# A hybrid attention and recurrence block: output gates computed in pairs, and sums and low parts of weights made by adding DMAs

## The chip, the cores and the metric

The kernel runs on one core of a Trainium2 chip. The core has four compute engines that run side by side, each with its own list of instructions executed in order: TensorE (PE, matrix products, results into eight PSUM banks), VectorE (DVE), ScalarE (ACT) and GpSimd (POOL). A fifth, SyncE (SP), issues DMAs here; ACT and POOL issue some too, and the DMA engines carry them out. An engine waits for another by a semaphore, and while its first instruction waits, everything behind that on the same engine waits with it. The metric is the time of one execution in microseconds (us); less is better.

## The reference

One layer over T = 528 tokens (16 learned ones and 512 of the input), width D = 2048, all in float32. In short:

```python
h = rms_norm(concat([meta, x]), norm_g)
q_a,k_a,v_a,z_a, q_i,k_i,w_i, q_b,f_b,i_b,z_b, gates = split(h @ w_in)
# branch A: an indexer scores keys per query, the top 128 are attended to
score = sum_h(relu(rope(q_i)_h @ rope(rms_norm(k_i))) * w_i_h)
sel   = top_k(where(chunk(key) <= chunk(query), score, -inf), 128)
y_a   = softmax_attention(rope(rms_norm(q_a)), rope(rms_norm(k_a)), v_a, sel) * silu(z_a)
# branch B: a gated linear recurrence (HGRN2), in chunks of 64
y_b   = rms_norm(hgrn2(silu(q_b), f, i_b)) * silu(z_b)
p     = stack([y_a, y_b]) @ w_branch            # per branch
out   = x + sum(sigmoid(gates) * p, branches) @ w_out
```

The product with `w_in` (2048 by 12368) is the largest piece, then `w_branch` and `w_out`.

## The kernel before

**Products.** TensorE takes float32 rounded to fewer bits (type fp32r). So each operand is split into a rounded high part and the low rest, and a product is three matmuls: high by high, high by low, low by high (`mm3`, L1606). Activations `hH`, `hL` stay in SBUF, 16 tiles each (one per 128 of D). Weights stream: SP loads chunks of 512 KB into six `raw` buffers; `hi_lo` (L402) makes `wh` on ACT (a rounding copy) and `wl` = `raw` − `wh` on DVE, three buffers of each. The number behind a name, as in `wh18`, counts chunks.

**Order of the work.** A head (L1616 on) loads x, normalises each block of 128 tokens (`norm_x`, L498: squares on ACT and DVE, a power on POOL), transposes it on PE (`px`), and makes `hH`, `hL`; with them run the first two jobs, kiwi (keys and weights of the indexer, 80 columns) and q_i block 0. While x arrives, PE runs 33 transposes of the identity into a bank `pw` that nobody reads.

Then *classical* blocks (`Job("in")`): 128 output columns, 16 tiles of D, three matmuls of 512 tokens each, 48 in all, weights in two chunks of 8 tiles. Before the change they are kiwi, eight q_i blocks and four z_a blocks (`NZA` = 4; z_a are the output gates of attention): chunks 0 to 25.

Then *pairs* (`run_pair`, L1263): two blocks of 128 columns at once by the seven-product scheme of Winograd and Strassen on halves of D and of the tokens. A pair has seven products of 24 matmuls of 256 (or 272) tokens, 168 in all; its weights are four chunks and sums of them: `s3` and `s4` by adding DMAs that POOL issues, `s2` and `s1` by DVE. The activations need sums too: `tops_task` (L1189) makes per pair of tiles k and 8+k `r1` = `hH`+`hL` and `r2` on DVE, then five more DVE sums and the splits into `tT`. `place_t3` (L1221) at last overwrites half of `hH`, `hL` with a sum and its low part. Pairs are, in order: 16 for HGRN, 2 for the other four z_a, 8 for attention, 16 for the merge gates. Then come branch jobs (32, `pg` at L95 with `yH`, `yL`) and output pairs (`po`).

**What sets the order.** Each engine's list is fixed when the program is written. Background work (the indexer's scores `psc`, `rl`, `score`; top-k; the tops; HGRN; attention) is written as generators, `tasks`. `pump` (L226) is called after each tile of a block and steps those whose planned ready time (`E.clk`, a rough model of the engines) has come, by priority, if SBUF slots (71, `room`) and PSUM banks (`bank`, `pair`) are free. `finish(t)` (L238) instead steps everything until `t` is done, without regard to what PE has to do meanwhile. It is called for the tops at the last classical block, ahead of its matmuls; behind that block's first chunk stands `place_t3`.

A score: PE makes `psc` from `kkH`, `kkL` and `qst` (a q_i block after its rotation on DVE and its split), ACT applies relu into `rl`, DVE adds it, weighted, to `score`. Each half block has four `psc` tiles of 144, 272, 400 and 528 keys; the last takes the one pair of banks. Each q_i block needs its own result first: ACT copies it (`xqi`), DVE rotates it (`qpx`, `qxc`), ACT and DVE split it into two `qst`.

In an attention head, `qa_task` (L826) ends with four exponentials and four scalings on ACT in one go, then `pv_task` (L896) multiplies with V. At the end of the last pair `finish_y`, `load_y` and `split_y` fetch the outputs `y` of branch B (`ORDER[0]` = 1) by eight ACT DMAs (`yr`) and split them (`yH` on ACT, `yL` on DVE).

Of the kernel before, what the change touches and what calls it, by code (L numbers as in the profile page):

```python
# [40 lines left out]
NZA = 4  # L41
# [144 lines left out]
def hybrid_kernel(ctx, tc, x, meta, vecs, w_in, rows, w_branch, w_out,  # L186
# [215 lines left out]
    def hi_lo(k, src, m, then=None, lazy=False):  # L402
        h = wp.tile([128, 1024], F32R, name=f"wh{k}", tag=f"wh{k % NWS}")
        l = wp.tile([128, 1024], F32R, name=f"wl{k}", tag=f"wl{k % NWS}")
        E.act(h[:, :m], src, AF.Copy)

        def lo():
            (E.ptt if k < 6 else E.tt)(l[:, :m], src, h[:, :m].bitcast(F32), OP.subtract)
            if then:
                then()  # L410

        if lazy:
            pend.append(lo)
        else:
            lo()
        return h, l

    def split_chunk(k, ch):
        load_upto(ch["i"])
        m = ch["nk"] * ch["ncols"]  # L420
        r, nk, n = ch["raw"], ch["nk"], ch["ncols"]
        ch["h"], ch["l"] = [], []
        if k < 4:
            for g in range(2):
                h, l = slot("eh", F32R), slot("el", F32R)
                w = 4 * n
                E.act(h[:, :w], r[:, w * g:w * g + w], AF.Copy)
                (E.ptt if k else E.tt)(l[:, :w], r[:, w * g:w * g + w], h[:, :w].bitcast(F32), OP.subtract)
                early.extend((h, l))
                ch["h"] += [h[:, n * i:n * i + n] for i in range(4)]  # L430
                ch["l"] += [l[:, n * i:n * i + n] for i in range(4)]
        else:
            h, l = hi_lo(k, r[:, :m], m)
            ch["h"] = [h[:, n * i:n * i + n] for i in range(nk)]
            ch["l"] = [l[:, n * i:n * i + n] for i in range(nk)]
        load_upto(ch["i"] + NRAW)
# [389 lines left out]
    def qa_task(h, xq, prev):  # L826
# [59 lines left out]
        yield e  # L886
        E.dve([sm], [sm], 4, lambda vv: vv.reciprocal(sm.rearrange("p (q i) -> p q i", i=4)[:, :, 3],
                                                      sm.rearrange("p (q i) -> p q i", i=4)[:, :, 2]))
        for qt in (3, 2, 1, 0):
            xs = ps[qt]  # L890
            e = E.act(xs[:, :KQ[qt]], xs[:, :KQ[qt]], AF.Copy, scale=col(qt, 3))
        pv_tasks.append(spawn(pv_task(h, ls, ps, e), 1))
# [3 lines left out]
    def pv_task(h, ls, ps, e):  # L896
# [23 lines left out]
        for b in (3, -1, 0, 1, 2):  # L920
# [32 lines left out]
            if b == 1:  # L953
# [234 lines left out]

    def tops_task():  # L1189
# [3 lines left out]
        for k in range(8):  # L1193
            yield from room(8 - k % 2)
            if k % 2 == 0:
                t3 = slot("t3")
            r1, r2, t1, c = slots("tr", 4)
            d = t3[:, 256 * (k % 2):256 * (k % 2) + 256]
            E.tt(r1[:, :512], hH[k][:, 16:528].bitcast(F32), hL[k][:, 16:528].bitcast(F32), OP.add)
            yield E.tt(r2[:, :512], hH[8 + k][:, 16:528].bitcast(F32), hL[8 + k][:, 16:528].bitcast(F32), OP.add)  # L1200
# [62 lines left out]
    def run_pair(pr, nxt, late, last):  # L1263
# [25 lines left out]
        for i, (wn, tn, bn, on_) in enumerate(SEVEN):  # L1289
# [55 lines left out]
            if last:  # L1345
                if i == 4:
                    S.put(*hH[:8], *hL[:8], *[t for k in range(8) for t in TB[k]["tiles"][:2]])
                    finish_y(ORDER[0])
                    ysplit = split_y(load_y(ORDER[0]), ORDER[0])
# [6 lines left out]
                if i > 4:  # L1356
                    for _ in range((4, 9)[i - 5]):
                        next(ysplit, None)
# [203 lines left out]
    jobs[3].pre = lambda: t_task.append(spawn(tops_task(), 2))  # L1562
# [22 lines left out]

    order = []
# [44 lines left out]
    for b, n in FIRST:  # L1631
# [40 lines left out]
    for ji, job in enumerate(jobs[2:], 3):  # L1672
        need[0] = 1 + jobs[ji].meta if ji < len(jobs) else 0
# [120 lines left out]
```

## Time and profile before

| | us |
|---|---|
| time, median of three runs | 1534.54 (1534.38 to 1535.71) |
| the profiled execution, its own time | 1537.39 |
| its span in the trace | 1535.6 |
| DVE busy | 1158.5 |
| ACT busy | 696.2 |
| POOL busy | 161.5 |
| granted clock of PE, mean | 0.998 |

How to read the profile: engines, then groups of instructions named by line, engine, operation and `out<-in` by the program's names. "Idle before" is the time for which an engine stood still just ahead of an instruction, and what ended it. Matmuls overlap in the pipeline, so the duration of one is longer than the distance between starts. In a table of windows each engine's busy time stands beside the count of its instructions, then the granted clock of PE (1.00 is full).

### The profile page before, as it was taken

The page shows a single profiled execution, that of the slowest core. Times are in us where ns is not written, and L with a number is a line of the kernel's source. Part 1 is how long each engine was busy: PE and PEld are TensorE (multiplying, and loading weights), DVE is VectorE, ACT ScalarE, POOL GpSimd, SP SyncE. Part 2 cuts the span into 40 slices and gives each one's busy share as a digit, 9 for nine tenths or more (in the row PEclk, how much of TensorE's full clock was granted, in tenths as well). Part 3 has the DMA queues.
Part 4 walks back from the last instruction along what each step waited for, and adds up shares of the span by engine and source line. Part 5 has one row for each costly group of instructions (what it writes and reads, how often), then busy time and mean ns, then how long its engine had stood idle before and what let it go on. Part 6 is the DMA issues. An engine that isn't in the chain of part 4 may idle for free.

```text
span 1535.6 us, 30559 instructions
## 1 busy us (share of the span) xinstructions
PE 1509.5 (98%) x12456; PEld 1427.7 (93%) x12456; DVE 1158.5 (75%) x1951; ACT 696.2 (45%) x1059; POOL 161.5 (11%) x174
## 2 busy tenths in 40 slices
PE   7999999999999999999999999999999999999998
PEld 6888889999999999999999999999999788889998
DVE  6699899999977787777767768768766444778665
ACT  5555444444444444434554554555443433434332
POOL 3100010010001001011101101101100000002221
PEclk9999999999999999999999999999999999999999
DMA  9222448766666585757667677677577664548783
GB/s 265 79 73 74 119 93 203 186 167 166 157 176 163 148 191 136 185 131 192 152 180 186 158 187 190 157 183 182 149 191 190 221 200 130 154 121 214 213 214 93
DMA packets 305276, 252.25 MB, mean 164 GB/s; under 512 B 11700, under 2 KB 266176, under 8 KB 305136
## 3 DMA queue, kind: packets, MB, share of 16 engines
q1 hardware_dynamic: 278688, 179.54, 40.0%
q0 software_dynamic: 14464, 52.52, 19.7%
q10 hardware_dynamic: 11984, 18.25, 3.8%
q8 instruction: 97, 1.59, 0.4%
q14 instruction: 43, 0.35, 0.1%
HBM read 169.11 MB, written 28.73 MB: 129 GB/s over the span
## 4 chain that ended last, share of the span: by engine, by line
PE 89%; DVE 6%; DMA 2%; issue 1%; ACT 1%; POOL 0%; ACTq 0%; SPq 0%; DVEq 0%; POOLq 0%
PE pg L95 18%; PE px L93 15%; PE pz L93 14%; PE po L93 10%; PE pv L93 7%; PE py L93 7%; PE pw L93 7%; DVE wl L109 2%; PE phl L95 1%; PE pov L93 1%; PE psc L95 1%; PE plg L95 1%; PE pho L95 1%; DVE tk L693 1%; PE px L99 1%
## 5 line engine op out<-in xcount | busy, mean ns | idle before, releaser
L103 ACT ACTIVATE wh<-raw 128x1024 fp32r<-128x1024 f32 x404 | 427.9, 1060 | 570.6 <-PE pz L93 138.8
L109 DVE TENSOR_TENSOR wl<-raw,wh 128x1024 fp32r<-128x1024 f32 x402 | 493.1, 1227 | 136.7 <-ACT wh L103 133.6
L93 PE MATMUL px<-hH,wh 128*128 128x272 f32 (+1 forms) x672 | 194.5, 289 | 1.3 <-ACT p L103 1.3
L93 PE MATMUL px<-hH,wl 128*128 128x272 f32 (+1 forms) x672 | 191.9, 286 | 0.0
L93 PE MATMUL px<-hL,wh 128*128 128x272 f32 (+1 forms) x672 | 191.9, 286 | 0.0
L118 POOL DMA_DIRECT2D raw<-raw x100 | 88.1, 995 | 981.4 <-DVE raw L109 616.9
L93 PE MATMUL po<-wh,mh 128*128 128x256 f32 x896 | 158.7, 281 | 0.5 <-DVE xq L109 0.5
L93 PEld LDWEIGHTS po<-wh,mh 128*128 128x128 f32 x896 | 137.4, 189 | 0.8 <-DVE xq L109 0.7
L93 PEld LDWEIGHTS px<-hH,wh 128*128 128x128 f32 x672 | 126.7, 189 | 2.1 <-ACT p L103 1.6
L93 PEld LDWEIGHTS px<-hL,wh 128*128 128x128 f32 x672 | 126.8, 189 | 0.0
L93 PEld LDWEIGHTS px<-hH,wl 128*128 128x128 f32 x672 | 126.6, 188 | 0.0
L93 PE MATMUL pw<-tT,wh 128*128 128x256 f32 x672 | 126.4, 287 | 0.0
L93 PE MATMUL po<-wl,mh 128*128 128x256 f32 x448 | 125.8, 281 | 0.0
L93 PE MATMUL pv<-tT,wh 128*128 128x256 f32 x672 | 125.1, 285 | 0.0
L93 PE MATMUL pz<-tT,wh 128*128 128x256 f32 x672 | 124.3, 284 | 0.0
L109 DVE TENSOR_TENSOR raw<-raw,raw 128x1024 f32<-128x1024 f32 x100 | 122.2, 1222 | 1.7
L93 PEld LDWEIGHTS pz<-tT,wh 128*128 128x128 f32 x672 | 103.1, 189 | 0.5
L93 PEld LDWEIGHTS pv<-tT,wh 128*128 128x128 f32 x672 | 103.0, 188 | 0.5
L93 PEld LDWEIGHTS pw<-tT,wh 128*128 128x128 f32 x672 | 103.0, 189 | 0.2
L95 PE MATMUL pg<-yL,wh 128*128 128x512 f32 x256 | 100.7, 394 | 2.0 <-DVE yL L109 2.0
L95 PE MATMUL pg<-yH,wh 128*128 128x512 f32 x256 | 100.9, 394 | 0.9 <-ACT yH L103 0.9
L95 PE MATMUL pg<-yH,wl 128*128 128x512 f32 x256 | 100.9, 394 | 0.0
(306 smaller groups left out, 3509.2 us busy)
## 6 DMA issues: line engine op xcount, KB each, us to landing
raw<-in_w_in_dram SPq DMA_DIRECT2D x192, 512.0 KB, 6.1
raw<-raw POOLq DMA_DIRECT2D x100, 512.0 KB, 5.9
raw<-in_w_branch_dram SPq DMA_DIRECT2D x32, 512.0 KB, 4.2
raw<-in_w_out_dram SPq DMA_DIRECT2D x32, 512.0 KB, 6.6
gd<-r SPq DMA_DIRECT2D x32, 256.0 KB, 2.2
gate<-gd SPq DMA_DIRECT2D x32, 256.0 KB, 4.4
held<-r SPq DMA_DIRECT2D x19, 264.0 KB, 3.2
held<-r SPq DMA_DIRECT2D x18, 256.0 KB, 2.0
```

The source lines that it names most:

```text
L93: self.nc.tensor.matmul(out, lhsT, rhs, start=start, stop=stop, skip_group_check=True)
L95: self.nc.tensor.matmul(out, lhsT, rhs, start=start, stop=stop)
L99: self.nc.tensor.transpose(out, in_, ident)
L103: self.nc.scalar.activation(out, in_, f, **kw)
L109: self.nc.vector.tensor_tensor(out, a, b, op=op)
L118: self.nc.gpsimd.dma_start(out, a, accum_op=OP.add)
L693: e = E.dve([w], [src, m8], kq, lambda v: v.match_replace(w, m8, src, NEG))
```

## The change

1. `NZA` 4 to 0. z_a blocks 0 to 3 become two more pairs (4 instead of 2). Classical blocks fall from 13 to 9, chunks 0 to 17; the last is now the last q_i block. Tops start one job earlier (`TAT` = 2).
2. `hi_lo(by="dma")`: for chunks 8 to 17 ACT writes `wl` = −`wh`, and an adding DMA that POOL issues adds `raw` to it. No DVE there.
3. `r1`, `r2` of the tops: POOL copies `hH` by DMA (`raw_h`), and an adding DMA adds `hL` (`add_h`), the copy for k+1 issued ahead.
4. The head: the copy `cvec` stands on ACT behind four steps of the norm instead of ahead; `el` of chunk 1 is made by DVE instead of POOL; four more identity transposes stand ahead of each of the tiles 0, 1, 2.
5. In attention, a yield behind every exponential and scaling, so that other work can be written between; `z` is fetched one step earlier in `pv_task`.
6. `y` of branch B: a background task `early_y` in place of the three calls at the end of the last pair.

```diff
-NZA = 4
+NZA = 0
+FILL = 4
+TD = 1
+LD = range(8, 24)
+TAT = 2
@@ hi_lo
         E.act(h[:, :m], src, AF.Copy)
+        if by == "dma":
+            E.act(l[:, :m], h[:, :m].bitcast(F32), AF.Copy, scale=-1.0)
+            E.dma_add(l[:, :m].bitcast(F32), src)
+            return h, l
@@ split_chunk
-                (E.ptt if k else E.tt)(l[:, :w], r[:, w * g:w * g + w], h[:, :w].bitcast(F32), OP.subtract)
+                (E.ptt if k > 1 else E.tt)(l[:, :w], r[:, w * g:w * g + w], h[:, :w].bitcast(F32), OP.subtract)
...
-            h, l = hi_lo(k, r[:, :m], m)
+            h, l = hi_lo(k, r[:, :m], m, by="dma" if k in LD and ch["job"].kind == "in" else "dve")
@@ qa_task
             e = E.act(xs[:, :KQ[qt]], xs[:, :KQ[qt]], AF.Exp, bias=col(qt, 1), accum_out=col(qt, 2))
-        yield e
+            yield e if qt == 0 else 0.0
...
             e = E.act(xs[:, :KQ[qt]], xs[:, :KQ[qt]], AF.Copy, scale=col(qt, 3))
+            yield 0.0
@@ pv_task
-            if b == 1:
+            if b == 0:
                 z = fetch("zs", zd[h], nc.scalar)
@@ tops_task
+    def raw_h(k):
+        r = RS[k] = slots("tr", 2)
+        for s, kt in zip(r, (k, 8 + k)):
+            nc.gpsimd.dma_start(s[:, :512], hH[kt][:, 16:528].bitcast(F32))
+            E.wr[s.tensor.name] = (E.clk["pe"] + 2500.0, "dma")
+
+    def add_h(k):
+        for s, kt in zip(RS[k], (k, 8 + k)):
+            E.dma_add(s[:, :512], hL[kt][:, 16:528].bitcast(F32))
...
+                if k not in RS:
+                    raw_h(k)
+                    add_h(k)
+                r1, r2, t1, c = *RS[k], *slots("tr", 2)
+                if k < 7 and len(S.free) >= 7:
+                    raw_h(k + 1)
+                yield ready(r1, r2)
+                if k + 1 in RS:
+                    add_h(k + 1)
...
-            E.tt(r1[:, :512], hH[k][:, 16:528].bitcast(F32), hL[k][:, 16:528].bitcast(F32), OP.add)
-            yield E.tt(r2[:, :512], hH[8 + k][:, 16:528].bitcast(F32), hL[8 + k][:, 16:528].bitcast(F32), OP.add)
@@ run_pair, last pair
-                    finish_y(ORDER[0])
-                    ysplit = split_y(load_y(ORDER[0]), ORDER[0])
...
-                if i > 4:
-                    for _ in range((4, 9)[i - 5]):
-                        next(ysplit, None)
@@ branch jobs
+    def early_y():
+        while not y_ready(ORDER[0]) or len(pv_tasks) < 8 or not all(t.done for t in pv_tasks):
+            yield WAIT
+        yield from room(18)
+        yield from split_y(load_y(ORDER[0]), ORDER[0])
@@ head
-    for i in range(33):
-        E.tr(pw[:, 0:128], ident, ident)
-    B1.put(pw)
-    E.act(cvec, pb[:, :35], AF.Copy)
-    B1.put(pb)
+    fill(33)
...
-    for b, n in FIRST:
+    for b, n in FIRST[:4]:
+        step(b, n)
+    E.act(cvec, pb[:, :35], AF.Copy)
+    B1.put(pb)
+    for b, n in FIRST[4:]:
         step(b, n)
...
         for kt in range(KT):
             prep_next()
+            if half == 0 and kt < 3:
+                fill(FILL)
+            elif half == 0 and kt == 3:
+                B1.put(pw)
```

What this does to the lists of the engines shows at three places. The numbers at the end of a name tell tiles of one name apart; the last columns are partitions by elements.

**PE, where the last classical blocks meet the scores.** Before, the last scores stand among the matmuls of a classical block (a z_a block, `pg`), a few at a time:

```order
L95 MATMUL psc_1950<-kkL_935,qst_1822 128x400
L95 MATMUL pg_1891<-hH_381,wh_1732 128x512
L95 MATMUL pg_1891<-hL_382,wh_1732 128x512
L95 MATMUL pg_1891<-hH_381,wl_1733 128x512
L95 MATMUL psc_1966<-kkH_934,qst_1822 128x264
L95 MATMUL psc_1966<-kkL_935,qst_1822 128x264
```

Now the matmuls of chunk 15 (the second half of the last but one q_i block, `pg_1546`) end, and 14 score tiles, 36 matmuls, stand in a row ahead of chunk 16 (`pg_1704`, the last q_i block). The row begins like this:

```order
L99 MATMUL pg_1546<-hH_548,wl_1484 128x512
L99 MATMUL psc_1698<-kkH_935,qst_1623 128x400
L99 MATMUL psc_1698<-kkL_935,qst_1623 128x400
L99 MATMUL psc_1714<-kkH_935,qst_1623 128x264
L99 MATMUL psc_1714<-kkL_935,qst_1623 128x264
```

and ends like this:

```order
L99 MATMUL psc_1805<-kkL_935,qst_1733 128x400
L99 MATMUL psc_1812<-kkH_935,qst_1733 128x264
L99 MATMUL psc_1812<-kkL_935,qst_1733 128x264
L99 MATMUL psc_1812<-kkH_935,qst_1733 128x264
L99 MATMUL psc_1812<-kkL_935,qst_1733 128x264
L99 MATMUL pg_1704<-hH_281,wh_1547 128x512
```

Seven of the 14 tiles (from the first that reads `qst_1732`, the fifth after `psc_1714`) belong to the block that chunk 15 has just finished. On DVE its rotation and its split stand like this now, with scores of the block ahead between them:

```order
L635 STREAM_SHUFFLE qpx_1705<-xqi_1701 128x512
L113 TENSOR_TENSOR qxc_1706<-xqi_1701,cq_114 128x512
L113 TENSOR_TENSOR qpx_1705<-qpx_1705,sq_115 128x512
L113 TENSOR_TENSOR qxc_1706<-qpx_1705,qxc_1706 128x512
L136 SCALAR_TENSOR_TENSOR score_942<-rl_1711,wi,score_942 128x400
L113 TENSOR_TENSOR tT_1720<-tr_1666,tT_1719 128x512
L113 TENSOR_TENSOR tT_1721<-tr_1667,tT_1721 128x256
L136 SCALAR_TENSOR_TENSOR score_941<-rl_1726,wi,score_941 128x528
L113 TENSOR_TENSOR qst_1732<-qxc_1706,qst_1732 64x512
```

So the scores of two blocks that stood among matmuls before now stand together ahead of the last block.

**ACT, between the last classical block and the first pair.** Before, `place_t3` (`hH` from a sum) stood between the splits of chunks 26 and 27, the first two of the pairs, and the last tops (`tT`) ahead of chunk 26:

```order
L103 ACTIVATE zs_2112<-pg_2024 128x512
L103 ACTIVATE tT_2120<-tr_2080 128x512
L103 ACTIVATE tT_2122<-tr_2081 128x256
L103 ACTIVATE wh_2130<-raw_1736 128x1024
L103 ACTIVATE hH_281<-t_82_912 128x256
```

Now the same pieces stand in the same order for chunk 18 (`wh_1840`), but right behind the row of scores:

```order
L107 ACTIVATE rl_1809<-psc_1805 128x400
L107 ACTIVATE rl_1818<-psc_1812 128x528
L107 ACTIVATE tT_1833<-tr_1827 128x512
L107 ACTIVATE tT_1835<-tr_1828 128x256
L107 ACTIVATE wh_1840<-raw_1240 128x1024
L107 ACTIVATE hH_281<-t_75_843 128x256
```

`tr_1827` there is the sum of two tiles that DVE makes from `tr_1821` and `tr_1822`. Those two, `r1` and `r2` of k = 7, now come over POOL's queue, as its rows show (`raw_1321<-raw_1240` is the sum s3 of the first pair):

```order
L122 DMA wl_1630<-raw_1172 128x1024
L122 DMA raw_1321<-raw_1240 128x1024
L1204 DMA tr_1821<-hH_417 128x512
L1204 DMA tr_1822<-hH_548 128x512
L122 DMA tr_1821<-hL_418 128x512
L122 DMA tr_1822<-hL_549 128x512
L122 DMA raw_1488<-raw_1321 128x1024
```

What moved: the splits that the first pair needs stand behind a chain of scores, a copying DMA, an adding DMA and DVE sums, which before stood a block or more ahead.

**ACT, where the pairs end and the branch jobs begin.** Before, behind eight DMA issues of `yr` (the last of them shown) came a chunk's split and then the splits of y:

```order
L1463 DMA yr_14500<-yd_7_139 128x512
L103 ACTIVATE wh_14536<-raw_14246 128x1024
L103 ACTIVATE yH_14543<-yr_14493 128x512
L103 ACTIVATE yH_14547<-yr_14494 128x512
L103 ACTIVATE yH_14551<-yr_14495 128x512
L103 ACTIVATE yH_14555<-yr_14496 128x512
L103 ACTIVATE wh_14583<-raw_14402 128x1024
```

Now three splits of y stand ahead of that chunk's:

```order
L1491 DMA yr_14756<-yd_7_139 128x512
L107 ACTIVATE yH_14765<-yr_14749 128x512
L107 ACTIVATE yH_14786<-yr_14750 128x512
L107 ACTIVATE yH_14796<-yr_14751 128x512
L107 ACTIVATE wh_14800<-raw_14498 128x1024
L107 ACTIVATE yH_14813<-yr_14752 128x512
L107 ACTIVATE wh_14835<-raw_14654 128x1024
```

The eight issues stand behind the same chunk's split as before (the second behind a pair's last `r`), so the loads themselves are not moved on ACT; three `yH` have moved ahead of one `wh`.

More of the change, by code (lines that the diff above doesn't have):

```diff
@@ L400, in flush, with hi_lo @@
             pend.pop(0)()
-    def hi_lo(k, src, m, then=None, lazy=False):
+    def hi_lo(k, src, m, then=None, lazy=False, by="dve"):
         h = wp.tile([128, 1024], F32R, name=f"wh{k}", tag=f"wh{k % NWS}")
@@ L1187, in hybrid_kernel @@
     TB = {}
+    RS = {}
+    def raw_h(k):
[6 more added lines that the diff above has]
+            E.dma_add(s[:, :512], hL[kt][:, 16:528].bitcast(F32))
     def tops_task():
@@ L1193, in tops_task @@
         for k in range(8):
-            yield from room(8 - k % 2)
+            yield from room(8 - k % 2 - 2 * (k in RS))
             if k % 2 == 0:
                 t3 = slot("t3")
-            r1, r2, t1, c = slots("tr", 4)
+            if TD:
+                if k not in RS:
[7 more added lines that the diff above has]
+                    add_h(k + 1)
+            else:
+                r1, r2, t1, c = slots("tr", 4)
+                E.tt(r1[:, :512], hH[k][:, 16:528].bitcast(F32), hL[k][:, 16:528].bitcast(F32), OP.add)
+                yield E.tt(r2[:, :512], hH[8 + k][:, 16:528].bitcast(F32), hL[8 + k][:, 16:528].bitcast(F32), OP.add)
             d = t3[:, 256 * (k % 2):256 * (k % 2) + 256]
-            E.tt(r1[:, :512], hH[k][:, 16:528].bitcast(F32), hL[k][:, 16:528].bitcast(F32), OP.add)
-            yield E.tt(r2[:, :512], hH[8 + k][:, 16:528].bitcast(F32), hL[8 + k][:, 16:528].bitcast(F32), OP.add)
             E.tt(t1[:, lo], r1[:, lo], r1[:, hi], OP.subtract)
@@ L1464, in load_y @@
         return yr
+    def early_y():
[3 more added lines that the diff above has]
+        yield from split_y(load_y(ORDER[0]), ORDER[0])
     def split_y(src, n):
         for h in range(8):
+            yield from room(2)
             yH[n, h], yL[n, h] = slot("yH", F32R), slot("yL", F32R)
@@ L1529, in f @@
             if p == 0:
-                if n == ORDER[1]:
-                    finish(splits[n])
-                else:
+                finish(splits[n])
+                if n == ORDER[0]:
                     load_gates(n, 0)
@@ L1555, in finish_y, with y_ready @@
             finish(t)
+    def y_ready(n):
+        return len(spills[n]) == 8 and all(t.done for t in spills[n])
     mask_t = []
-    nclass0 = 9 + NZA // 2
+    nclass0 = 7 if NZA < 4 else 9 + NZA // 2
     jobs = [Job("in", C_KI, 80, True, done=d_kiwi)]
@@ L1561, in hybrid_kernel @@
     jobs += [Job("in", C_ZA + 128 * j, 128, done=d_za(j)) for j in range(NZA)]
-    jobs[3].pre = lambda: t_task.append(spawn(tops_task(), 2))
+    jobs[TAT].pre = lambda: t_task.append(spawn(tops_task(), 2))
     jobs[6].pre = lambda: spawn(consts(), 2)
@@ L1584, in hgrn_pairs @@
                 (C_IB + 128 * h, C_ZB + 128 * h, NM, ((copy, r_ib(h)), (silu, r_zb(h))))]
+    splits[ORDER[0]] = spawn(early_y(), 3)
     order = []
@@ L1619, in hybrid_kernel, with fill @@
     pw = B1.get("pw")
-    for i in range(33):
-        E.tr(pw[:, 0:128], ident, ident)
-    B1.put(pw)
-    E.act(cvec, pb[:, :35], AF.Copy)
-    B1.put(pb)
+    def fill(n):
+        for i in range(n):
+            E.tr(pw[:, 0:128], ident, ident)
+    fill(33)
     gens = {b: norm_x(b) for b in (0, 1, 2, 3, "m")}
@@ L1672, in hybrid_kernel @@
     for ji, job in enumerate(jobs[2:], 3):
-        need[0] = 1 + jobs[ji].meta if ji < len(jobs) else 0
+        need[0] = 1 + (jobs[ji].meta > 0) if ji < len(jobs) else 0
         if job.pre:
```

## The prediction

> **What bounds the kernel now.** I read the page first, then PE's waits, then tables of windows, to see whether anything but PE sets the end.
>
> ```profile
> span 1535.6 us, 30559 instructions
> PE 1509.5 (98%) x12456; PEld 1427.7 (93%) x12456; DVE 1158.5 (75%) x1951; ACT 696.2 (45%) x1059; POOL 161.5 (11%) x174
> PE 89%; DVE 6%; DMA 2%; issue 1%; ACT 1%; POOL 0%; ACTq 0%; SPq 0%; DVEq 0%; POOLq 0%
> ```
>
> PE is busy for 1509.5 of 1535.6 us and makes 89% of the chain that ended last. So a gain is PE work that goes, or some of the 26 us in which PE stands still. The table of PE's waits (total us, times, longest) names:
>
> ```profile
> PE pc L99 <- DMA vrow<-in_vecs_dram: 8.0, 1, 8.0
> PE pz L93 <- DVE r L109: 2.3, 2, 1.4
> PE py L93 <- DVE wl L109: 2.0, 1, 2.0
> PE px L93 <- ACT p L103: 1.3, 1, 1.3
> PE pg L95 <- DVE yL L109: 2.0, 2, 1.2
> PE px L99 <- DVE xm L125: 0.9, 1, 0.9
> PE pg L95 <- ACT yH L103: 0.9, 1, 0.9
> PE pg L95 <- POOL el L113: 0.8, 1, 0.8
> ```
>
> Beside the 8.0 us for the first load they are single and short. Windows show where DVE, 75% busy on average, is close to full (columns: length, then busy time and count of PE, PE's loads, DVE, ACT, POOL, then PE's granted clock, the DMA share, GB/s):
>
> ```profile
> 80.00:200.00 120.00, 120.00 (x590) 101.50 (x589) 112.85 (x222) 65.14 (x124) 0.93 (x1) 1.00 0.31 84
> 187.17:198.26 11.09, 11.09 (x49) 9.01 (x48) 10.92 (x26) 6.01 (x13) 0.00 (x0) 1.00 0.26 72
> 200.00:204.00 4.00, 2.00 (x16) 1.80 (x15) 4.00 (x11) 0.45 (x2) 0.00 (x0) 1.00 0.16 62
> 208.00:212.00 4.00, 3.78 (x32) 3.58 (x31) 3.96 (x7) 2.96 (x4) 2.44 (x3) 1.00 0.67 125
> 216.00:220.00 4.00, 3.13 (x27) 2.96 (x26) 3.97 (x7) 1.74 (x2) 0.00 (x0) 1.00 1.15 306
> ```
>
> From 80 to 200 us, the classical blocks, PE never stands, though DVE works 112.85 of 120 us. Where the pairs begin, PE lacks 2.00, 0.22 and 0.87 us: 3.1 us, with DVE full. Two consequences: taking work off DVE in the classical stretch gains nothing there by itself, and the change is decided at the seam between classical blocks and pairs.
>
> **A. Two more pairs for four classical blocks.** The second window of those above is one classical block, 48 matmuls of 512 in 11.09 us. The chain that ended last, in a stretch of pairs, lists products of 24 matmuls:
>
> ```profile
> 1145.54 2.84 PE pw L93 x24
> 1148.38 2.84 PE pz L93 x24
> 1151.22 2.85 PE px L93 x24
> ```
>
> A pair is seven of them, 7 x 2.845 = 19.9 us, and does the work of two blocks, 22.2 us. Four blocks go (44.4 us), two pairs come (39.8): **−4.5 us**. The new pairs' sums and splits are those of the 42 pairs now there, and these run PE without a gap in most stretches, so I add nothing.
>
> **B. The head.** Around the first tiles:
>
> ```profile
> 14.37 0.23 PE L99 MATMUL px<-ident,xm 16*128 16x16 f32 x1 [0.90 <-DVE xm L125]
> 17.92 0.49 PE L95 MATMUL pg<-hH,el 128*128 128x256 f32 x1 [0.83 <-POOL el L113]
> 8.30 0.20 ACT L103 ACTIVATE cvec<-pc 128x35 f32<-128x35 f32 x1 [6.08 <-PE pc L99]
> 10.00:11.00 1.00, 1.00 (x6) 1.00 (x5) 0.21 (x2) 0.97 (x3) 0.58 (x1) 1.00 1.15 302
> 12.00:13.00 1.00, 1.00 (x12) 1.00 (x11) 0.97 (x4) 0.97 (x5) 0.76 (x1) 1.00 1.21 278
> 18.00:20.00 2.00, 2.00 (x9) 1.74 (x10) 1.75 (x5) 0.49 (x1) 1.27 (x1) 0.51 1.00 326
> 22.00:24.00 2.00, 2.00 (x10) 1.74 (x9) 1.64 (x4) 0.41 (x2) 0.00 (x0) 0.50 1.16 305
> 26.00:28.00 2.00, 2.00 (x16) 1.74 (x15) 1.09 (x3) 1.38 (x4) 1.68 (x3) 1.00 0.45 104
> ```
>
> ACT sits behind `cvec` until 8.30, so the squares of the norm start late; moved behind four steps they start as x arrives, and the wait of 0.90 us at `px` goes. `el` of chunk 1 on DVE (0.48 us a piece there, 1.4 on POOL) removes the 0.83. And after these two waits the clock is at half from 18 to about 24.7 us (0.51, 0.50), in which a tile takes 2.15 us, against 1.26 once it is at 1.00 (counts 10 and 16 in 2 us show the same ratio); if it stays up, three tiles gain 0.9 each, 2.7 us. Twelve identity transposes cost 12 x 1/12 us (the window 12 to 13 holds 12 of them) = 1.0 us, half of it inside a wait that is there anyway. **B = −0.9 − 0.8 − 2.7 + 0.7 = −3.7 us** if the clock holds, −1.0 if not. I take the first: the transposes themselves went from 6 to 12 a microsecond while PE ran nothing else, so here they do count as work for the clock. The Trainium skill, "TensorE: Matmul & The Clock Gate", Part 4, says the opposite: full clock does not engage for transposes, which would leave B at −1.0; the two windows speak against it, but do not show whether four transposes a tile suffice.
>
> **C. The seam.** Here the order of the rows shows two new chains. Prices:
>
> ```profile
> L103 ACT ACTIVATE xqi<-pg 128x512 f32<-128x512 f32 x8 | 4.7, 591 | 3.2 <-PE pg L95 3.2
> L627 DVE STREAM_SHUFFLE qpx<-xqi 128x512 f32<-128x512 f32 x8 | 5.9, 735 | 0.0
> L109 DVE TENSOR_TENSOR qxc<-qpx,qxc 128x512 f32<-128x512 f32 x8 | 5.5, 692 | 0.3
> L132 DVE SCALAR_TENSOR_TENSOR score<-rl,wi,score 128x528 f32<-128x528 f32 x15 | 11.4, 762 | 0.1
> L132 DVE SCALAR_TENSOR_TENSOR score<-rl,wi,score 128x400 f32<-128x400 f32 x15 | 9.4, 629 | 0.0
> L109 DVE TENSOR_TENSOR qst<-qxc,qst 64x512 fp32r<-64x512 f32 x16 | 11.0, 686 | 0.6
> L109 DVE TENSOR_TENSOR wl<-raw,wh 128x1024 fp32r<-128x1024 f32 x402 | 493.1, 1227 | 136.7 <-ACT wh L103 133.6
> raw<-raw POOLq DMA_DIRECT2D x100, 512.0 KB, 5.9
> held<-r SPq DMA_DIRECT2D x18, 256.0 KB, 2.0
> ```
>
> First, 14 score tiles stand in a row on PE between chunks 15 and 16. Their 36 matmuls are 4.8 us of work at 231 ns per 512 columns. The fifth after `psc_1714` reads `qst_1732`, made from chunk 15's own result: `xqi` 0.6, the shuffle and three DVE operations 2.8, then on DVE a score of 400 (0.6), two `tT` (1.1 by the same width as `qst` and half of it), a score of 528 (0.8), `qst` 0.7: 6.6 us after chunk 15. PE has 1.6 us of tiles until there, so it waits about 5. Of the remaining tiles those of 528 share one pair of banks, and each `rl` waits for a slot that a `score` leaves; following these row by row, I get the last tile done 11.4 us after chunk 15. Of this 4.8 are work: **+6.6 us**. The least is 2.5 (`xqi`, rotation and `qst` alone, 4.1, less 1.6), if what stands between on DVE is done early.
>
> Second, the tops of k = 7 end on POOL's queue: `tr_1822` waits for a slot of a late score (about 12.7 us after chunk 15), then copy, addition, four DVE sums (1.7), `tT` on ACT (1.0), `wh18` 1.1, `wl18` 1.2. The trace before has no copy or addition of 256 KB on POOL: the nearest rows are 2.0 us (256 KB from SP) and 5.9 (512 KB added by POOL); I take 4 and 5, nearer to POOL's. That gives `wl18` at about 26.5; PE, through chunks 16 and 17 (11.1 us), asks for it at about 22.8: 3.7 us, with both ends of the landings 0 to 6.5. Behind `wh18` eight `hH` stand ahead of `wh19` as before, for some 2.5 us more in the next products. All of this is 6.6 + 3.7 + 2.5 = 12.8, less the 3.1 us that the seam costs now: **C = about +9 us**, from +1 to +15.
>
> Costed at nothing: chunks 8 to 17's lows by DMA. Each adds an ACT pass (1.06 us; ACT worked 65 of 120 us in the stretch), an issue on POOL and a landing of 5.9, about 10 us in all against a lead of 12 us or more that three buffers give at 5.5 us a chunk. POOL's queue is in order: a tops addition that waits for its copy holds a low behind it. If the cover is gone, a low late by 1 to 3 us shows at once as a PE wait; I put in +0.5.
>
> **D. Attention.** In the table of waits `pz<-r` (its longest, 1.4) and `px<-p` (1.3) stand in the attention part just behind ACT's four exponentials and scalings, which now let a split in between. I take **−1.5 us** of these 2.7, between 0 and −2.7; a softmax that is spread out delays V's product, but that has other heads' work as cover.
>
> **E. y of branch B.**
>
> ```profile
> 1185.31 5.02 ACTq L1463 DMA_DIRECT2D yr<-yd  x8
> 1190.43 1.06 ACT L103 ACTIVATE wh<-raw 128x1024 fp32r<-128x1024 f32 x1 [4.07 <-DMA yr<-yd]
> 1193.73 0.50 PE L95 MATMUL pg<-yL,wh 128*128 128x512 f32 x1 [1.18 <-DVE yL L109]
> ```
>
> The eight issues hold ACT for 5 us and are still where they were; PE then loses about 2.9 us in three waits (0.90 for `yH`, 2.0 for `yL` in all). Three `yH` now stand ahead of one `wh` of 1.06 us, so the first `yL` comes about 1.2 earlier: **−1.2 us** (−2.9 to +1, since the later `yH` come behind more splits).
>
> **Sum.** −4.5 − 3.7 + 9 + 0.5 − 1.5 − 1.2 = −1.4 us, made against the profiled execution (1537.39; span 1535.6 and 1.8 around it), which lies 2.9 above the median shown. On the median, 1534.54 − 1.4 = **1533.1 us**. 0.2%, 3.1 us, is about what a measurement of this kernel tells from no change.
>
> **Rivals.** *R1, the seam stays cheap.* If `qst` is ready early and POOL's transfers land at the low end, C is +1: total −9.4, 1525.1 us. For it: DVE loses 10 lows (12.3 us) and 16 sums (10.9) ahead of the seam. Against: it also loses 44 us of PE time behind which to work, so its load per block does not fall. *R2, slower: the long wait costs the clock.* A wait of 5 us is longer than any in the trace behind the start. If the clock falls to half as it did at 18 us, for 6.7 us, chunk 16 loses 3.4, and with both landings at 5.9 C is 9 + 3.4 + 2.8 = 15: total +4.6, 1539.1. It decides once C is over about +13.5. For it: waits of 0.9 and 0.83 were followed by half clock in the head. Against: 2.0 us at the seam left it at 1.00, so the length alone does not tell. The Trainium skill, same page, "Why this matters for your kernels", warns of PE-idle gaps over about 3 us; the trace before has no such gap in mid-kernel to test it. *R3, the fillers do not hold the clock*: B −1.0, total +1.3, 1535.8. That the lows by DMA are late throughout is in its range.
>
> **Chances.** Forecast 0.34, R1 0.26, R2 0.25, R3 0.15. Faster than 1531.5: 0.11 + 0.25 + 0 + 0.02 = 0.38. Slower than 1537.6: 0.03 + 0 + 0.20 + 0.04 = 0.27. Within: 0.35. The forecast's own range is 1530 to 1536.5; as R1 and R2 hold half of the chance, the range runs from 1524 to 1541.
>
> **What would show it.** A: four blocks of 11.1 us fewer ahead of the first pair, and pairs that still take 19.9. B: PEclk 1.00 between 18 and 24 us, no wait of `px` for `xm` or of `pg` for `el`. C: PE's waits list `psc` waiting for DVE `qst` with about 5 us, then `py` or `px` for `wl` with 3 to 4. R2: a PEclk under 1 behind the first. D: `pz<-r` and `px<-p` shorter. E: `pg<-yL` about 1. Wrong altogether would be waits of `pg` for `wl` between 80 and 150 us, which I cost at 0.5.

## The result, and the profile after

The changed kernel is slower: 1548.91 us median (1548.02 to 1550.83) against 1534.97 (1534.38 to 1535.71) for the kernel before in the same runs, a ratio of 1.0088 (95% interval 1.0076 to 1.0101), +13.9 us. I had forecast 1533.1 and a range up to 1541. The two profiled executions differ less, by 11.9 us, as the one of the kernel before (1537.39) lies above its median: executions of that kernel on record run from 1533.40 us at a mean clock of 0.999 to 1539.44 at 0.997. The page of the profiled execution after (span, busy time, clock by fortieths of the span) and PE's waits (total us, times, longest):

```profile
span 1547.5 us, 31010 instructions
PE 1513.9 (98%) x12612; PEld 1435.0 (93%) x12612; DVE 1154.0 (75%) x1947; ACT 714.8 (46%) x1079; POOL 197.8 (13%) x218
PEclk9998999999999999999999999999999999999999
```

```profile
PE pc L103 <- DMA vrow<-in_vecs_dram: 6.9, 1, 6.9
PE pz L97 <- DVE r L113: 5.0, 3, 3.8
PE psc L99 <- DVE qst L113: 4.6, 1, 4.6
PE phl L103 <- DMA v<-held: 2.1, 2, 1.4
PE phd L99 <- ACT hk L107: 1.7, 2, 0.9
...
PE psc L99 <- ACT rl L107: 1.5, 1, 1.5
PE phl L99 <- DVE QA L113: 1.0, 3, 0.3
PE pg L99 <- DMA wl<-raw: 0.9, 1, 0.9
```

The forecast wait of `psc` for `qst` is there. The others were not forecast: a wait of 3.8 us for `r`, and three kinds in the HGRN heads (`phl`, `phd`), where before only `phd` stood with 0.6. To see where the time went I cut both traces at the starts of the same matmuls (end of the fourth tile, last classical matmul, each pair's first `py`, first branch matmul, first `po`). Lengths in us; "work" is what the matmuls added or taken away are worth by the prediction's own rates (231 ns per matmul of 512, 19.9 us per pair):

| stretch | before | after | difference | of it work |
|---|---|---|---|---|
| head, four tiles | 25.2 | 21.6 | −3.6 | |
| classical blocks | 172.9 | 138.8 | −34.1 | −44.4 |
| to the second pair's `py` | 27.3 | 26.4 | −0.9 | |
| HGRN and z_a pairs | 411.2 | 458.5 | +47.3 | +39.8 |
| attention pairs | 190.5 | 192.9 | +2.4 | |
| gate pairs | 346.8 | 345.7 | −1.1 | |
| last pair | 18.2 | 22.6 | +4.4 | |
| branch jobs | 180.3 | 178.6 | −1.7 | |
| output | 163.2 | 162.3 | −0.9 | |

The sum is +11.8 us; the spans differ by 11.9. Of the head's −3.6, 1.1 us has nothing to do with the change: the first load, for which PE waits, landed at 6.9 us in this execution and at 8.0 in the one before (in the other traces of this document at 6.9 to 8.6). The seam costs −34.1 + 44.4 − 0.9 = +9.4, the y transition 4.4 − 1.7 = +2.7, the HGRN and z_a stretch 47.3 − 39.8 = +7.5 beyond its two pairs. Of these 7.5, 0.9 is work: eight matmuls (`phv`, `pht`) that stood in the attention stretch before. PE's named waits between the second pair and attention rose by 5.4, from 0.6 to 6.0 us: 2.1 for tiles fetched back from memory (`v<-held`), 1.7 for `hk`, 1.2 for `r`, 1.0 for `QA`.

The seam and the head, in windows after (columns as in the prediction's windows; the first one lies in the head):

```profile
18.00:20.00 2.00, 2.00 (x18) 1.71 (x16) 1.24 (x4) 0.49 (x1) 0.00 (x0) 1.00 1.04 390
135.00:140.00 5.00, 1.17 (x9) 0.84 (x7) 4.78 (x10) 2.99 (x7) 0.00 (x0) 1.00 1.06 241
140.00:145.00 5.00, 2.79 (x10) 2.26 (x10) 3.56 (x9) 2.40 (x7) 0.00 (x0) 0.55 0.50 141
145.00:150.00 5.00, 4.99 (x18) 4.70 (x19) 5.00 (x13) 2.95 (x7) 2.11 (x3) 0.50 0.18 72
150.00:155.00 5.00, 5.00 (x21) 4.02 (x21) 1.20 (x4) 0.00 (x0) 1.04 (x2) 0.92 0.70 139
```

In the head the clock is at 1.00 where it was at 0.51, and 18 instructions of PE end in 2 us instead of 9. At the seam PE works 1.17 of 5 us, and behind the wait of 4.6 us the clock is at half for about 10 us: the last scores and the first matmuls of chunk 16 run slowly.

The y transition, in the timeline after (start, duration, instruction, idle time before it and its releaser), from ACT, DVE and PE:

```profile
1195.39 4.89 ACTq L1491 DMA_DIRECT2D yr<-yd  x8
1200.33 1.67 ACT L107 ACTIVATE yH<-yr 128x512 fp32r<-128x512 f32 x3 [3.88 <-DMA yr<-yd]
...
1200.99 0.69 DVE L113 TENSOR_TENSOR yL<-yr,yH 128x512 fp32r<-128x512 f32 x1 [3.28 <-ACT yH L107]
1201.60 0.41 DVE L113 TENSOR_TENSOR r<-p,pz 128x256 f32<-128x256 f32 x1
...
1202.16 0.55 PE L97 MATMUL pz<-hH,wh 128*128 128x256 f32 x1 [3.84 <-DVE r L113]
```

Here it can be read from bottom to top. The last product of the last pair needs the bank that DVE empties into `r`; on DVE `yL` stands ahead of `r`; `yL` waits for `yH` on ACT, and that for the loads, whose eight issues occupy ACT for 4.9 us. Before, `r` stood ahead of `yL`. Behind this wait of 3.84 us the clock fell too, and PE ended 6 instructions in a microsecond where it later ends 9:

```profile
1203.00:1204.00 1.00, 1.00 (x6) 1.00 (x6) 1.00 (x2) 0.46 (x1) 0.00 (x0) 0.50 1.11 365
1206.00:1207.00 1.00, 1.00 (x9) 0.95 (x8) 0.00 (x0) 0.35 (x1) 0.00 (x0) 1.00 0.91 269
```

The first 15 matmuls of this product took 3.34 us instead of some 1.8 (at full clock 24 take 2.84 us), so about 1.6 us of the y transition is the clock.

### The profile page after: what moved, and what is told of

Same layout as the page of the kernel before. It is cut to its first block, busy times and chain, and to the rows that moved or that the text cites. A ratio compares the mean times of both kernels' runs of the same rounds, so it can differ in the third digit from the quotient of the medians.

```text
span 1547.5 us, 31010 instructions
## 1 busy us (share of the span) xinstructions
PE 1513.9 (98%) x12612; PEld 1435.0 (93%) x12612; DVE 1154.0 (75%) x1947; ACT 714.8 (46%) x1079; POOL 197.8 (13%) x218
## 5 line engine op out<-in xcount | busy, mean ns | idle before, releaser
L107 ACT ACTIVATE wh<-raw 128x1024 fp32r<-128x1024 f32 x410 | 434.1, 1060 | 610.3 <-PE pz L97 142.2
L97 PE MATMUL px<-hH,wh 128*128 128x272 f32 (+1 forms) x704 | 203.7, 289 | 0.1
L97 PE MATMUL px<-hL,wh 128*128 128x272 f32 (+1 forms) x704 | 201.2, 286 | 0.0
L97 PE MATMUL px<-hH,wl 128*128 128x272 f32 (+1 forms) x704 | 200.8, 285 | 0.0
L97 PEld LDWEIGHTS px<-hH,wh 128*128 128x128 f32 x704 | 132.9, 189 | 1.1 <-ACT p L107 0.5
L97 PEld LDWEIGHTS px<-hH,wl 128*128 128x128 f32 x704 | 132.8, 189 | 0.0
L97 PEld LDWEIGHTS px<-hL,wh 128*128 128x128 f32 x704 | 132.6, 188 | 0.0
L97 PE MATMUL pz<-tT,wh 128*128 128x256 f32 x704 | 129.7, 284 | 0.0
L97 PE MATMUL pz<-hH,wh 128*128 128x256 f32 x352 | 102.7, 292 | 5.1 <-DVE r L113 5.0
L97 PE MATMUL py<-hH,wh 128*128 128x256 f32 x352 | 101.2, 288 | 0.0
```

Source lines behind the costliest of these rows:

```text
L97: self.nc.tensor.matmul(out, lhsT, rhs, start=start, stop=stop, skip_group_check=True)
L107: self.nc.scalar.activation(out, in_, f, **kw)
```

## The experiments

Times are medians; "before" is the kernel before, run beside the kernel in question. Its median moved between 1534.80 and 1536.41 us from one group of runs to the next, so a difference to the changed kernel (1548.91) or to head_only (1534.95) in another group is good to about 1.5 us. Kernels that run the same matmuls as another are compared by the stretches of the table above.

**The old y in the changed kernel.** The edit:

```diff
+                    finish_y(ORDER[0])
+                    ysplit = split_y(load_y(ORDER[0]), ORDER[0])
...
-    splits[ORDER[0]] = spawn(early_y(), 3)
```

> The changed kernel with the loading and splitting of y put back as before the change (three calls in the last pair, no background task). Theory 1: the 3.8 us wait of the last product pz for DVE r comes from DVE standing behind yL, whose load is only on its way; with the old order it goes and the three short waits of before (2.9 us) return: about 1546.5 us, 2 to 3 less than the changed kernel. Rival: DVE is late there for another reason (transfers of the seam or the gates), and the time stays within 1 us of 1548.9.

1548.68 us (1547.29 to 1554.27), no change. Last pair and branch jobs took 20.2 + 181.7 = 201.9 us against 201.2 in the changed kernel and 198.5 before. But the eight issues took longer in this run:

```profile
1194.69 7.05 ACTq L1496 DMA_DIRECT2D yr<-yd  x8
1201.84 1.06 ACT L107 ACTIVATE wh<-raw 128x1024 fp32r<-128x1024 f32 x1 [6.09 <-DMA yr<-yd]
```

7.05 us where it was 5.02 before and 4.89 after, so this run could not price the order of y; h_y below does.

**Four classical z_a blocks in the changed kernel** (`NZA = 4`).

> The changed kernel with four z_a blocks classical again (NZA 4); head, adding DMAs, softmax and y stay as changed. Theory 1: the row of scores, its wait of 4.6 us and the half clock behind it go, the seam of before (3.1 us) shrinks as DVE has less to do, head gains 3.6, y costs 2.7: 1531 to 1534 us, and the excess in the stretch of HGRN pairs falls back to about 18.5 us. Rival (the adding DMAs disturb loads, POOL and DVE everywhere): the excess in that stretch stays at 23 or more and the time is over 1537.

1550.34 us (before 1536.41): the rival's time, but not its mechanism, since za4_dve below leaves the adding DMAs out and is no faster. PE's waits:

```profile
PE pz L97 <- DVE r L113: 8.6, 6, 4.6
...
PE pg L99 <- DMA wl<-raw: 3.9, 2, 3.1
PE pka L103 <- DMA xk<-held: 3.6, 2, 2.0
PE phl L103 <- DMA v<-held: 2.3, 2, 1.3
```

The seam was cheap (24.0 us to the second pair's `py`), but classical blocks, HGRN and attention took 6.7, 3.8 and 4.4 us more than before. So z_a in pairs is not the whole cause: something else in the change loses as much.

**The opening alone, on the kernel before.**

```diff
-                (E.ptt if k else E.tt)(l[:, :w], r[:, w * g:w * g + w], h[:, :w].bitcast(F32), OP.subtract)
+                (E.ptt if k > 1 else E.tt)(l[:, :w], r[:, w * g:w * g + w], h[:, :w].bitcast(F32), OP.subtract)
...
+    for b, n in FIRST[:4]:
+        step(b, n)
+    E.act(cvec, pb[:, :35], AF.Copy)
...
+            if half == 0 and kt < 3:
+                fill(4)
...
```

> The kernel before with the changed opening alone (fillers, cvec behind four steps, el of chunk 1 on DVE). Theory 1: the gain of 3.6 us in the head is kept to the end: 1531.4 us. Rival: the program behind it is reordered or later waits give it back: within 1 us of 1535.

1534.95 us, the rival's number, but against 1536.41 beside it: ratio 0.9990 (0.9981 to 1.0000). In the profile the head took 22.6 us for 25.2, and all stretches behind it the lengths of before within 0.4 us. The first load landed here at 7.8 us, close to the 8.0 of before, so this pair of traces prices the opening best: −2.6 us, kept to the end. The medians show 1.5 of it, with an interval that just reaches no change.

**The forced end of the tops behind chunk 16.**

```diff
-        if ji == nclass:
-            finish(t_task[0])
...
             if ji == nclass and ch["k0"] == 0:
+                finish(t_task[0])
                 place_t3(0)
```

> The changed kernel with the forced end of the tops moved from ahead of the last classical block to behind its first chunk. The rotation of chunk 15's block then has 5.5 us of matmuls beside it. Theory 1 (the wait is that chain): the 4.6 us wait and the half clock go, in part given back since the last tops and hH, hL now have one chunk less of cover: 1541 to 1547. Rival (the row is limited by DVE and the slots, wherever it stands): the wait moves behind chunk 16 and the time is 1548 to 1553.

1553.11 us, at the upper end of what the rival said: the wait for `qst` was still 3.4 us, and the first pair now waited for its split.

```profile
PE pz L97 <- DVE r L113: 9.0, 3, 7.8
...
PE py L97 <- ACT wh L107: 3.5, 1, 3.5
PE psc L99 <- DVE qst L113: 3.4, 1, 3.4
```

The first wait at the seam is 1.2 us shorter for it, and a new one of 3.5 takes its place. (In this run the issues of y took 8.85 us, which is where the wait of 7.8 for `r` is from; classical blocks and seam together took 2.2 us more than in the changed kernel.)

**Less top-k.** `range(TOPK // 8)` became `range(2)`; the kernel leaves out 14 of 16 rounds of the selection.

> The changed kernel with 2 instead of 16 rounds of the top-k per block of queries; that part of the selection is left out, and DVE has about 45 to 50 us less to do between the seam and 400 us. Theory 2 (with NZA 0 the top-k's DVE work runs 44 us deeper into the HGRN pairs, and the products and HGRN steps there wait for DVE): the excess of PE over its own work in the stretch of HGRN and z_a pairs falls from 25 us to 18 or less, time about 1540. Rival (the waits come from where the planner put HGRN's steps, or from loads): the excess stays at 23 to 26, time 1547 to 1549.

1544.52 us (a single execution), between the two. The HGRN waits `phl` and `phd` of 4.8 us in all became 1.0 (for `q<-held`), but the stretch of HGRN and z_a grew from 458.5 to 462.8 us, since other background work moved into it; beyond the work so moved it became about 2 us shorter, not 7. With 4.4 us less in all, DVE's backlog explains a part at most.

**All lows and tops sums on DVE.** `TD = 0`, `LD = range(0)`.

> The changed kernel with all low parts and tops sums on DVE again, no adding DMAs for them. Theory A (the adders relieve DVE and are worth it): the row of scores at the seam is longer (20 tiles instead of 14 by the order), DVE is full, and the time is 1552 to 1558. Rival B (the adding DMAs themselves are late and crowd the queues): the waits of pg for wl (0.9 and 0.4) and the extra waits for held loads go, and the time is 1542 to 1547.

1560.03 us: theory A, and 2 more than its range. Without the adders the wait for `qst` was 8.5 us and `px` waited 2.9 for `wh`. With the order that goes with them, the adding DMAs are worth 11 us, 6.7 of it in the classical blocks and at the seam (139.3 + 32.6 us against 138.8 + 26.4). My cost of them was +0.5; the one wait of `pg` for such a `wl` that the table above names is 0.9 us.

**The old softmax in the changed kernel** (the yields of the diff taken out, `z` back at `b == 1`).

> The changed kernel with the exponentials and scalings of attention in one go and the z fetch where it was. My step D: the excess in the attention and gate stretches rises by 1.5 us (14.2 now), time 1550. Rival (the spread softmax delays V's products): it falls by 2 us to the 12 of before, time 1546.5.

1558.22 us, 9 more than the changed kernel, far beyond either number; attention took 196.9 us instead of 192.9. In its timeline ACT, and then PE:

```profile
760.96 0.40 ACT L107 ACTIVATE r<-px 128x272 f32<-128x272 f32 x1 [8.61 <-DMA held<-r]
...
761.41 0.80 PE L97 MATMUL pw<-tT,wh 128*128 128x256 f32 x2 [3.99 <-ACT r L107]
```

ACT's copy of a product waited 8.6 us for a tile whose spill had not landed, and PE 4.0 for ACT.

**Two classical z_a blocks** (`NZA = 2`).

> The changed kernel with two z_a blocks classical (NZA 2), three z_a pairs. By the order only 10 score matmuls stand in a row there, instead of 36. Theory 1 (the seam's row is what NZA 0 costs): the excess of classical and first pair falls from 15.2 to under 8, 2.2 us of the pairs' gain stay, time 1540 to 1544. Rival (za_classical's losses come with any classical z_a block under these edits): 1548 to 1551.

1562.93 us, worse than both. Classical blocks now cost only about 2 us extra, but the first pair waited:

```profile
PE px L97 <- ACT wh L107: 11.2, 1, 11.2
...
PE py L97 <- DVE wl L113: 3.1, 1, 3.1
PE px L97 <- DVE wl L113: 2.7, 1, 2.7
...
172.28 1.01 ACT L107 ACTIVATE rl<-psc 128x400 f32<-128x400 f32 x2 [6.88 <-DMA zd<-zs]
```

On DVE the last tops stood behind six rounds of top-k (9.3 us), and these behind scores whose `rl` waited on ACT for 6.88 us: a DMA that writes a z_a block out had to land first (last line, from ACT's timeline). What I saw as the scores' row is one face of a deadline: splits for the first pair stand in line behind whatever was written first.

**Transposes in the seam's wait.**

```diff
                     pb = yield from bank("psc")
+                    if (j, i, qt) == (6, 0, 0):
+                        c = dict(E.clk)
+                        for _ in range(42):
+                            E.tr(pb[:, 0:128], ident, ident)
+                        E.clk.update(c)
```

> The changed kernel with 42 transposes of the identity on PE right ahead of the score tile that waits 4.6 us at the seam (nobody reads them; they end about when its operand is there). Theory 1 (the idle wait, not the work behind it, lets the clock fall to half from about 141 to 150.6 us): the clock stays at 1.00 and the last scores and the start of chunk 16 gain 2 to 3 us: 1546 to 1547, about 2.5 less. Rival (the clock falls anyway, as transposes do not count): the same 1549 within 1 us.

1546.19 us (1543.67 to 1547.29), 2.7 less, the time of theory 1; in the traces classical blocks and seam are 1.8 us shorter. The transposes and a later wait in the timeline, and the same windows as above:

```profile
135.59 4.75 PE L103 MATMUL psc<-ident 128*128 128x128 f32 x42
140.51 0.33 PE L99 MATMUL psc<-kkH,qst 128*128 128x144 f32 x1 [0.17 <-DVE qst L113]
...
143.60 0.39 PE L99 MATMUL psc<-kkH,qst 128*128 128x264 f32 x1 [1.50 <-ACT rl L107]
```

```profile
140.00:145.00 5.00, 3.33 (x24) 2.62 (x21) 4.46 (x14) 2.64 (x8) 0.34 (x1) 1.00 0.43 117
145.00:150.00 5.00, 4.35 (x15) 3.50 (x14) 4.54 (x10) 2.48 (x6) 1.72 (x3) 0.66 0.28 107
150.00:155.00 5.00, 5.00 (x23) 4.08 (x23) 0.89 (x3) 0.00 (x0) 0.87 (x1) 1.00 0.59 104
```

The clock held through the 4.75 us of transposes, but not to the end: behind two waits of the scores for `rl`, 1.50 and 0.65 us, it was at half from about 146.2 to 149.4 us (0.66 in the second window). That is some 3 us of half clock instead of 10.

**Head, softmax and y alone, and in pairs, around the kernel before.** za4_dve is the changed kernel with `NZA = 4`, `TD = 0`, `LD = range(0)`; za4_dve_sm has the old softmax too; head_softmax is head_only with the softmax edit.

> The changed kernel with four classical z_a blocks and all low parts and tops sums on DVE; left of the change are the head, the softmax yields with the z fetch, the background y, and the earlier start of the tops. If the adding DMAs cost time once the z_a blocks are classical (za_classical 1550.3, with 8.7 us of excess in the classical stretch): that excess falls to 2 to 3 and the time to 1535 to 1541. Rival (the loss of za_classical is in softmax and y): it stays at 1547 or more.

> As za4_dve, with the softmax and the z fetch as before the change: head, background y and the earlier tops remain. Theory E (the background y costs 2 to 4 us at the end of the pairs): head_only plus 2 to 4, 1537 to 1539, all of it in the last pair. Rival: equal to head_only, 1535.

> The kernel before with the changed opening and with the softmax yields and the earlier z fetch. My step D (1.5 us less in attention): 1533.4. Rival from sm_old's side (in the changed kernel the yields are worth 5 us or more because there a burst met the pairs badly, not in general): 1535 within 1, or slower if attention's excess of 5.0 rises as tasks shift.

1551.87, 1556.21 and 1543.13 us: the first as its rival said, the other two far above every number expected. The softmax edit, a gain of 4 in one setting (za4_dve against za4_dve_sm) and of 9 in another (sm_old), costs 8 us on the order of before: attention 196.3 us instead of 190.5, in part because key tiles are now asked for ahead of their landing:

```profile
PE pka L99 <- DMA xk<-held: 3.5, 2, 1.9
```

And za4_dve, with neither adders nor new pairs, lost 17 us, and za4_dve_sm, without the softmax edit, 21. The background y is worth 1.5 to 2.7 of these (h_y below). That left two causes for the rest: the earlier tops, or any change of the order.

> The kernel before with the changed opening (head_only, 1534.95) and the tops started one job earlier, nothing else. Cause 1 (the earlier tops disturb what follows): the excess in the HGRN stretch rises from 18.9 to 25 or more, as in za4_dve, time 1543 to 1550. Rival (the loss of za4_dve needs the softmax or y edits too): 1535 to 1537.

```diff
-    jobs[3].pre = lambda: t_task.append(spawn(tops_task(), 2))
+    jobs[2].pre = lambda: t_task.append(spawn(tops_task(), 2))
```

1552.68 us: the tops one job earlier, alone, cost 18 us on head_only, more than cause 1 said.

> head_only with the planner's margin 350 instead of 300: the same work, background steps written 50 ns later, some 260 of PE's rows in other places. Cause 2 (the order before is a fitted one, and any other costs): 3 to 10 us more, 1538 to 1545, as excess in the stretches of HGRN, attention and gates. Cause 1: within 1.5 us of 1535.

`MARGIN` 350.0 instead of 300.0. 1547.28 us, 12 more than head_only and more than cause 2 said, with the same instructions. No edit of the change is in it besides the head. PE's waits:

```profile
PE pz L93 <- DVE r L109: 5.2, 4, 1.8
PE px L93 <- ACT p L103: 2.7, 2, 1.3
PE py L93 <- DVE wl L109: 2.5, 1, 2.5
PE phl L99 <- DMA v<-held: 2.1, 1, 2.1
```

> The changed kernel with the planner's margin 350 instead of 300, the same work. Cause 2: the excess in HGRN, attention and gates moves by several us either way with the seam untouched, anywhere from 1543 to 1556. Cause 1: within 1.5 us of 1549.

1553.82 us, 5 more than the changed kernel, as cause 2 said; its HGRN and z_a stretch grew from 458.5 to 463.8. Five kernels with the same matmuls (but for the transposes of the opening) side by side, lengths in us:

| stretch | before | head_only | head_softmax | h_m350 | h_tat2 |
|---|---|---|---|---|---|
| classical | 172.9 | 172.9 | 173.0 | 172.9 | 178.2 |
| to the second `py` | 27.3 | 26.9 | 26.9 | 28.5 | 23.4 |
| HGRN and z_a | 411.2 | 411.2 | 411.2 | 415.3 | 420.3 |
| attention | 190.5 | 190.5 | 196.3 | 193.9 | 198.1 |
| gates | 346.8 | 346.7 | 348.7 | 348.7 | 346.6 |

Only the place of background rows on the engines' lists differs from head_only, and it is worth 8 to 18 us.

**The background y alone, on head_only.**

> head_only with the background y, nothing else; the order of PE's rows is unchanged. Theory E: yL now stands on DVE ahead of the last product's sums, and PE waits there for the loads: 2 to 3 us at the end of the pairs, 1537 to 1538. Rival (my forecast, a gain of 1.2): 1533.7.

1536.45 us, 1.5 over head_only (before 1534.8 beside it), a little under theory E's range, with PE's wait for `r` up from 2.3 to 6.5:

```profile
PE pz L93 <- DVE r L109: 6.5, 3, 4.2
```

In the traces last pair and branch jobs take 201.9 us against 199.2, +2.7, the same as in the changed kernel: theory E.

**The loads of y issued by POOL.**

```diff
-            (nc.sync if n == ORDER[1] else nc.scalar).dma_start(yr[h][:, :512], yd[n][h])
+            (nc.sync if n == ORDER[1] else nc.gpsimd).dma_start(yr[h][:, :512], yd[n][h])
```

> head_only with the eight loads of y issued by POOL instead of ACT; the order of PE's rows is unchanged. If the waits at the end of the pairs (4.7 us of excess in last pair and branch) come from ACT standing behind the issues: yH and yL start at the landing, and 1 to 2.5 us go: about 1533 to 1534, under the kernel before. Rival (the landing of the loads decides, 5.5 us after their issue, POOL's issues not being quicker): within 0.7 us of head_only's 1535.

> The changed kernel with the 42 transposes at the seam and the loads of y issued by POOL. If the issues on ACT are what DVE's yL and the last product wait for: 1546.2 less 1 to 3, 1543 to 1545. Rival: 1546 to 1547, as in seam_fill.

On head_only: 1532.83 us against 1535.31 for the kernel before, ratio 0.9984 (0.9975 to 0.9993). This version is 0.16% faster than the kernel before. In the changed kernel with the transposes: 1541.21 us, 5.0 under seam_fill where I expected 1 to 3, with the long wait for `r` gone. In h_ypool POOL's issues, then ACT:

```profile
1172.48 3.77 POOL L1463 DMA_DIRECT2D yr<-yd  x7
1178.05 0.54 POOL L1463 DMA_DIRECT2D yr<-yd  x1 [1.81 <-DMA raw<-raw]
...
1184.74 1.06 ACT L103 ACTIVATE wh<-raw 128x1024 fp32r<-128x1024 f32 x1 [1.78 <-PE pw L93]
1185.70 2.18 ACT L103 ACTIVATE yH<-yr 128x512 fp32r<-128x512 f32 x4
```

POOL was not quicker, the eight took 6.1 us there. But it had only one issue ahead of them, so the first came some 10 us earlier than on ACT in head_only (1182.35), and `yH` found its data. Last pair and branch jobs took 196.3 us for head_only's 199.2.

## Why the prediction was wrong

**A, two pairs for four blocks (−4.5): right.** PE's matmuls of 512 in `pg` fell by 192, and a pair with nothing beside it still took 19.9 us.

**B, the head (−3.7): right in kind, too large by 1.2.** The −3.6 of the trace agree by luck, as 1.1 of them are the first load's earlier landing; counted from there the head took 14.7 us instead of 17.2, −2.5, and head_only says the same. R3's time is out: the clock is at 1.00 from 18 us on. (In the sum the fillers stand with 0.7, where the sentence before gives half of 1.0.)

**C, the seam (+9 and +0.5): right in sum (+9.4), not in its parts.** I gave 6.6 to the row of scores and 6.2 to the tops behind it, less the 3.1 of the seam before, which is 9.7 and went into the sum as 9. The row took from 134.3 to 148.5, 14.2 us for 4.8 of work, 9.4 too long: 6.1 of waits (4.56 for `qst`, 1.49 for `rl`), as forecast, and about 3.3 from the half clock, which cost chunk 16 another 1 us. The tops came to nothing, since PE was late itself: `wl18` ended 24.5 us after chunk 15 (I had 26.5). So the clock took the place of the tops.

Of R2 the mechanism was there (about 4.4 us of half clock behind a wait of 4.6 us, R2 had 3.4; seam_fill wins 2.7 of it back), but not the landings. That row and seam both come to 9.4 is chance: the seam's figure is net of the 3.1 us and holds some 2 us from elsewhere in the classical blocks. That transposes keep the clock up, which the Trainium skill, "TensorE: Matmul & The Clock Gate", Part 4, denies, is shown by seam_fill, where it stayed at 1.00 through 4.75 us of them. The head doesn't show it, since the two waits of 0.90 and 0.83 us went together with the new transposes.

**E, y (−1.2): wrong, +2.7.** The step that failed is "three `yH` now stand ahead of one `wh`": I read ACT's list and not DVE's. There `yL` had moved ahead of `r`, on which the last product waits, and the clock fell behind that wait. h_y shows the same +2.7 with this edit alone. I also took the issues for a fixed 5 us; the eighteen profiles in which ACT issues them show 4.6 to 8.9.

**D, the softmax (−1.5): wrong.** Attention and gates together took 1.3 us more, with 0.9 of work moved out of them. The two waits that I meant to remove did go: neither is left in these stretches. But waits of V's product `pov` there rose from 0.9 to 2.6 us, the cost that I had called covered. And the edit has no price of its own: it costs 8 us on the order of before (head_softmax), while taking it out of the changed kernel costs 9 (sm_old).

**What failed most is "I add nothing".** The step said that the new pairs' sums and splits run as those of the 42 pairs now there, and stopped at the seam. The HGRN and z_a stretch lost 7.5 us beyond its two pairs. I had costed the edits one by one against the waits of the trace before, as if the rows in between kept their places. For the head and the y edit PE's list does keep its order; the fewer classical blocks, the earlier tops and the softmax yields move hundreds of rows of background work. A new order alone can cost as much: 12 us by a constant of the planner in the kernel before, 5 in the changed kernel, 18 for the tops one job earlier. New pairs are not needed for it: the same stretch lost 3.8 us in za_classical and 9.8 in za4_dve, which have the old number of pairs. Every other order of the background tried on the kernel before (head_softmax, h_m350, h_tat2) was slower; that the order before is one fitted to this chip is my reading of that. The waits that come are for `held`, `r`, `hk`, `p`; that the planner misses them because its model of loads and landings is rough is not shown.

What stays open: which moved row causes which of the 7.5 us. No run kept the order of HGRN with four z_a pairs, and none took the earlier start of the tops, which cost 18 us on head_only, out of the changed kernel; how much of the 7.5 is its doing is not known. That they come from lost fit is the reading that the runs support, and topk_short puts a part (about 2) on DVE's backlog; it isn't shown row by row.

## What to carry to other kernels

Where a planner or priorities write the order, price a change by its new order as a whole: run a version in which only the order moves (a margin, a start one job earlier), and see how much that alone is worth, before any edit is credited or blamed. Read a moved instruction on each engine's list that it shares, and ask who stands behind it there. Issue loads from an engine that has nothing to do, ahead of the place where their data is needed.

## What the runs showed of the hardware

Eight load issues of 256 KB on ACT took 5.02, 5.28, 4.89, 7.05 and 8.85 us in before, head_only, the changed kernel, y_old and finish_late, though the issues are the same; their traces show no other instruction of ACT starting between them. On POOL they took 6.1 us (h_ypool) and 6.4 (with the transposes, in the changed kernel), of which 1.8 is a gap ahead of the last. Adding DMAs of 512 KB for the lows landed in 5.4 to 10.0 us (median 7.6), longer than the 5.9 of the pairs' sums before.

The clock fell to half after a wait of 4.6 us at the seam and after one of 3.84 at the last product, and stayed up through 2.0 at the old seam. With PE kept at transposes for 4.75 us it stayed at 1.00, but then fell behind waits of 1.50 and 0.65, as it was at half behind 0.90 and 0.83 in the head of before. So in these traces the length of a single wait does not tell whether the clock falls. Nor does the column of the clock tell it at the start: in the prediction's windows it is 1.00 from 10 to 11 us, where PE ended 6 transposes in a microsecond, and 1.00 from 12 to 13, where it ended 12.
